# A four-layer fp32 decoder trunk on one core: outputs of a state-space block moved into the gated product, and masked attention products of both halves made ahead

## The chip, the core and the metric

The kernel runs on one core of a Trainium2 chip. The core has five engines with their own instruction queues: TensorE (PE, matrix products; its weight loads are shown as PEld), VectorE (DVE), ScalarE (ACT), GpSimd (POOL) and SyncE (SP, which only issues transfers here). They meet through semaphores; PE writes to PSUM, where this kernel keeps eight tiles of 128 x 512 fp32; all else lies in SBUF or in the chip's memory. The metric is the device time of one execution in microseconds. Before the change the median of three runs is 1496.48 us (1496.17 to 1499.66).

## The reference

256 positions of width 1024 pass four layers. Each layer is `h += mixer(rmsnorm(h))`, then `h += relu(rmsnorm(h) @ w1)**2 @ w2` of width 4096, then `h += (p[i] @ ple_proj) * sigmoid(rmsnorm(h) @ ple_gate)`, the embedding step. The mixers are S5, forgetting attention (FoX), gated linear attention (GLA), and S5 again. All is fp32.

S5, cut to what matters:

```python
u = xn @ w_in                              # 64 groups of 16 channels, 64 complex states each
h[t] = a * h[t-1] + bbar @ u[t]            # diagonal, complex, per group
y[t] = Re(C @ h[t]) + d_skip * u[t]
z1, z2 = split(gelu(y) @ w_glu)            # 1024 -> 2 x 1024
out = (z1 * sigmoid(z2)) @ w_out
```

GLA works in four chunks of 64 positions, four heads:

```python
att = where(causal, q_dec @ k_inv.T, 0)    # in the chunk
o = att @ v + q_dec @ state
state = exp(b_last) * state + k_upd.T @ v
out = (rmsnorm(o) * gn * silu(r)) @ w_out
```

## The kernel before

**Dense products.** An fp32 operand is split into a high and a low part (type fp32r in the trace); a product is three matmuls (hi hi, hi lo, lo hi). Weights come in units of 512 KB: SP loads `raw` (a ring of 3 buffers), ACT rounds it to `whi`, DVE subtracts to `wlo` (rings of 4), and PE makes 24 matmuls of 128x256 of it (lines 172 to 174).

**S5** works on four blocks of 256 channels. For block b the step letters are: `w` the input product, `u` and its rearrangement U by 8 small transfers (`s5_inputs`); `i` the block's tables (rotation `rot`, input weights `win`) and the decay; `o` the way out (`qo`), the lag products `pk` (lines 917 to 922, PSUM tag mk), their copy `kk` by ACT, and four transfers that spread it to the lag matrix `tm` (line 932, queue of ACT in the first S5); `s` the state: products of U (line 967, 64x64 matmuls, in pairs for the two halves of the partitions), then on DVE rotations, two scans and the terms P and W (lines 980 to 989); `y` the outputs (`s5_outputs`): py (tag po) sums U against tm (line 1000), P and W against qo (line 1004), then ACT's gelu G (line 1007), four transposes into pg (line 1010), and the split into the two parts of `gT[b]` (lines 266 and 267). `p` is the layer's embedding product, of nothing but inputs.

The first S5 makes its tables in place and keeps P and W apart; the last one fetches tables that were made ahead in earlier layers (`kept`) and adds W into P on DVE (lines 987 to 989). After the steps comes the gated product of gT with `s_w_glu`: for each half, four units of the right columns (sigmoid by ACT), then four of the left. The first S5 runs from 0 to some 188 us, GLA from some 780 to 885, the last S5 from some 1125 to 1260.

**What sets the order.** The strings FIRST and LATER set the program order of the steps. The framework then reorders the instructions of each engine by its own estimate of when their inputs are ready; within an engine they run in the order so found. `issue_after` holds an instruction behind another: the gated product's `wlo` is held behind `lo_after`, the last state row W of the latest block. PSUM is shared by tags with a ring each: acc 3, wk 3, po 1, mk 1; a tile waits until the one before it in the ring has been read. mk holds both the lag products and the transposes of the outputs.

**GLA.** For each half (two chunks): pa = masked products (line 648, 16 records in the trace), `att` from it (POOL's memset, line 650; DVE's predicated copy, line 651), then for both pairs of heads po = att v (line 661) + q state (line 663), and the state update pu (line 669, DVE 675). The square sums of po go by ACT (681) and POOL (682, 683) to DVE's o (686).

Of the kernel before, what the change touches and what calls it, by code (L numbers as in the profile page):

```python
# [13 lines left out]
ALU = mybir.AluOpType  # L14
# [3 lines left out]
T, D, FF, DEPTH = 256, 1024, 4096, 4  # L18
# [4 lines left out]
        "acc": 3, "wk": 3, "po": 1, "mk": 1}  # L23


FIRST = "f0 w0 o0 w1 i0 w2 w3 f1 s0 i1 o1 s1 f2 i2 y0 o2 s2 y1 f3 i3 o3 s3 y2 p0 y3"
LATER = "w0 i0 o0 w1 i1 o1 w2 s0 i2 w3 s1 y0 o2 s2 i3 y1 o3 s3 y2 p3 y3"

HELD = 2

# [28 lines left out]
class Trunk:  # L59


    def __init__(self, ctx, tc, A):
        self.tc, self.nc, self.A = tc, tc.nc, A
        nc = self.nc
# [4 lines left out]
        self.dram = pool("dram", bufs=1, space=bass.MemoryType.DRAM)  # L69
        self.sm = pool("sm", bufs=4)  # L70
        self.pp = pool("pp", bufs=4, space=PSUM)
        self.kept = self.ahead = self.last_unit = self.lo_after = None
        self.pp_done = {}
        P = 128
        const = lambda name, shape, dt=F32: self.const.tile(shape, dt, name=name)
# [72 lines left out]
    def unit(self, src, nk, nc_, scale=None):  # L148

        nc = self.nc  # L150
        raw = self.wp.tile([128, nk, nc_], F32, name="raw", tag="raw", bufs=BUFS["raw"])
        self.last_unit = nc.sync.dma_start(raw, src.rearrange("(k p) n -> p k n", p=128))
        hi = self.wp.tile([128, nk, nc_], F32R, name="whi", tag="wh", bufs=BUFS["wh"])
        lo = self.wp.tile([128, nk, nc_], F32R, name="wlo", tag="wl", bufs=BUFS["wl"])
        if scale is None:
            nc.scalar.copy(hi, raw)  # L156
            with self.tc.issue_after(self.lo_after.ins) if self.lo_after else nullcontext():
                self.last_lo = nc.vector.tensor_tensor(lo, raw, hi.bitcast(F32), ALU.subtract)  # L158
        else:
            nc.scalar.mul(hi, raw, scale)  # L160
            nc.vector.scalar_tensor_tensor(lo, raw, scale, hi.bitcast(F32), ALU.mult, ALU.subtract)
        return hi, lo
# [412 lines left out]
    def gla(self, l):  # L575
        nc, A = self.nc, self.A
        NH, DK, DV = 4, 128, 256
        x = self.scaled(l)
# [8 lines left out]
        r = self.rstd(rows)  # L587
# [15 lines left out]
        last = chunks(cum)[:, :, :, 63:64]  # L603
# [35 lines left out]
        self.dense(x, A["gla_w_in"], key, (1,), tags=("acc", "wk"))  # L639
        state = [self.a2("state", (128, 2, DV)) for b in range(2)]  # L640
        os = [[None, None], [None, None]]
        for half in range(2):
            pa = self.psum((128, NH, 64))
            for h in range(NH):
# [4 lines left out]
            at = self.t2("att", (128, NH, 64))  # L649
            nc.gpsimd.memset(at, 0.0)  # L650
            nc.vector.copy_predicated(at, self.causal.bitcast(mybir.dt.uint8), pa)
            for b in range(2):
                po = self.psum((128, 2, DV))
                for c in range(2):
                    cs = slice(c * 64, (c + 1) * 64)
                    ts = slice(half * 128 + c * 64, half * 128 + (c + 1) * 64)
                    first = half == 0 and c == 0
# [9 lines left out]
                    for hh in range(2):  # L667
                        h = 2 * b + hh
                        nc.tensor.matmul(pu[:, hh, :], ku[half][cs, h * DK:(h + 1) * DK], v[half][b][cs, hh * DV:(hh + 1) * DV],
                                         start=True, stop=True)  # L670
# [285 lines left out]
    def s5_states(self, b, U, win, rot, d0, split):  # L956

        nc = self.nc
        V = nc.vector
# [21 lines left out]
        if split:  # L981
            V.memset(W[:, :, :, 0:1], 0.0)
            V.tensor_tensor(W[:, 0, :, 1:64], r[:, 1], s, ALU.mult)
            self.lo_after = V.scalar_tensor_tensor(W[:, 1, :, 1:64], r[:, 0], -1.0, s, ALU.mult, ALU.mult)
            return U, [[P[:, i], W[:, i]] for i in range(2)]
        w = W[:, :, :, 1:64]
        V.tensor_tensor(w, r, s.unsqueeze(1).broadcast_to([128, 2, 8, 63]), ALU.mult)
# [4 lines left out]
    def s5_outputs(self, b, U, terms, out, tm, gT):  # L992

        nc = self.nc

        py = self.psum((128, 8, 64), "po")
        gs = [slice(g * 64, (g + 1) * 64) for g in range(2)]
        for p in range(8):
            for g in range(2):
                nc.tensor.matmul(py[gs[g], p, :], U[gs[g], p, :], tm[gs[g], p], start=True, stop=False, skip_group_check=True)  # L1000
            for i in range(2):
                for n, t in enumerate(terms[i]):
                    for g in range(2):
                        nc.tensor.matmul(py[gs[g], p, :], t[gs[g], p, :], out[i][gs[g], :, p], start=False, stop=i == 1 and n == len(terms[i]) - 1,
                                         skip_group_check=True)
        G = self.t2("G", (128, 4, 8, 16))
        nc.scalar.activation(G, py.rearrange("x p (i c) -> x i p c", i=4), AF.Gelu_apprx_tanh)
        pg = self.psum((128, 2, T), "mk")
        for i in range(4):
            nc.tensor.transpose(pg[:, :, i::4], G[:, i].rearrange("x p c -> x (p c)"), self.ident)  # L1010
        self.split(pg, gT[b][:, :, 0], gT[b][:, :, 1])
# [29 lines left out]
    def s5(self, l):  # L1041
# [71 lines left out]

        for t in (FIRST if first else LATER).split():
            step(t[0], int(t[1]))
        if first:
            self.masks()
        m = self.ktiles("glu", tag="m4")
        for b in range(2):
            sg = [None, None]  # L1120

            def right(n, ps):
                sg[n % 2] = self.f2("sg")
                nc.scalar.activation(sg[n % 2], ps, AF.Sigmoid)

            def left(n, ps):
                t = sg[n % 2]
                nc.vector.tensor_tensor(t, ps, t, ALU.mult)
                self.split(t, m[n][:, :, 0], m[n][:, :, 1])

            self.dense(gT, A["s5_w_glu"][j], right, (b + 2,))
            self.dense(gT, A["s5_w_glu"][j], left, (b,))
        self.lo_after = None
        self.out_proj(m, A["s5_w_out"][j])

    def final(self, out):
# [96 lines left out]
```

## Time and profile before

| | |
|---|---|
| median of 3 runs | 1496.48 us (1496.17 to 1499.66) |
| profiled execution | 1498.76 us, of it the span 1497.0 us |
| mean granted TensorE clock | 0.971 of full |
| busy: PE, PEld, DVE, ACT, POOL | 95%, 85%, 70%, 48%, 6% |
| instructions | 26616 |
| memory traffic | 242.68 MB read, 7.86 MB written, 167 GB/s over the span |

The span goes from the first to the last instruction of the profiled execution. In a timeline a row is a run of like instructions: start, busy time, engine, line, operation, tiles written and read, shape, count; in brackets stands how long the engine had idled before and what ended it. An fp32 matmul shows as two records. Waits are put down to the event that came last. An answer by stretches gives, for each, its length, then busy time and instruction count of the engines, the granted clock, the share of the transfer engines and GB/s.

### The profile page before, as it was taken

Reading aid. Unit: us, or ns where it says so; the run is one execution under the profiler, and the core shown is the slowest. Engines: PE = TensorE matmul, PEld = TensorE weight load, DVE = VectorE, ACT = ScalarE, POOL = GpSimd, SP = SyncE. Lnnn points to the kernel's source line nnn. Section 1 sums busy time; section 2 is a strip of 40 time slices with the busy share of each in tenths; the row PEclk is TensorE's granted clock in tenths of the full one; section 3 lists DMA queues with packets and bytes.
Section 4 is the critical chain, followed back from the end, with each engine's and each line's share of the span. In section 5 each row is a group of like instructions: output and inputs, shape, how many; then the busy total and the mean of one; then the engine's idle time right before and its main releaser. Section 6 shows DMA issues by size and latency. Waiting matters only on the chain.

```text
span 1497.0 us, 26616 instructions
## 1 busy us (share of the span) xinstructions
PE 1416.0 (95%) x10734; PEld 1273.0 (85%) x10734; DVE 1055.2 (70%) x1739; ACT 721.3 (48%) x1118; POOL 85.7 (6%) x142
## 2 busy tenths in 40 slices
PE   8767999999999999999999999999999699999998
PEld 7656998888999888887999568888899699888898
DVE  8973477786776678886776528887666956766765
ACT  3212455455565555454567425545554244554444
POOL 3100000000100000010004000000000000000020
PEclk9979999999999999999999969999999899999999
DMA  6503565556645446775564415676576445566562
GB/s 223 167 13 92 185 184 180 180 173 228 186 138 158 141 127 188 247 232 183 182 186 137 154 43 182 220 230 205 170 247 200 123 138 176 169 204 187 169 197 71
DMA packets 146347, 255.06 MB, mean 170 GB/s; under 512 B 24768, under 2 KB 35296, under 8 KB 146224
## 3 DMA queue, kind: packets, MB, share of 16 engines
q1 hardware_dynamic: 132912, 234.35, 50.8%
q0 software_dynamic: 5248, 17.31, 3.5%
q10 hardware_dynamic: 8064, 1.71, 0.6%
q8 instruction: 84, 1.38, 0.4%
q14 instruction: 39, 0.32, 0.1%
HBM read 242.68 MB, written 7.86 MB: 167 GB/s over the span
## 4 chain that ended last, share of the span: by engine, by line
PE 82%; DVE 8%; DMA 4%; ACT 3%; issue 2%; ACTq 0%; POOL 0%; SPq 0%; DVEq 0%; POOLq 0%
PE wk L208 11%; PE acc L208 9%; PE acc L172 6%; PE acc L173 6%; PE acc L174 6%; PE wk L210 5%; PE acc L210 4%; PE wk L172 4%; PE wk L173 4%; PE wk L174 4%; PE mk L208 3%; PE po L208 3%; DVE wlo L158 2%; PE mk L210 2%; PE po L210 1%
## 5 line engine op out<-in xcount | busy, mean ns | idle before, releaser
L158 DVE TENSOR_TENSOR wlo<-raw,whi 128x1024 fp32r<-128x1024 f32 x406 | 494.8, 1228 | 305.3 <-ACT whi L156 298.7
L156 ACT CAST whi<-raw 128x1024 fp32r<-128x1024 f32 x406 | 422.1, 1049 | 464.7 <-PE acc L173 85.0
L208 PE MATMUL wk<-x,whi 128*128 128x512 f32 x576 | 181.2, 399 | 8.3 <-DVE relu L219 8.3
L210 PEld LDWEIGHTS wk<-x,wlo 128*128 128x128 f32 x576 | 106.3, 189 | 23.1 <-issue 0.2
L208 PE MATMUL acc<-s,whi 128*128 128x512 f32 x384 | 118.8, 395 | 0.0
L210 PE MATMUL wk<-x,wlo 128*128 128x256 f32 x576 | 112.9, 280 | 0.0
L172 PE MATMUL acc<-x,whi 128*128 128x256 f32 x352 | 99.6, 288 | 4.6 <-DVE u L1051 2.9
L208 PEld LDWEIGHTS wk<-x,whi 128*128 128x128 f32 x576 | 91.2, 190 | 11.9 <-DVE relu L219 9.2
L173 PE MATMUL acc<-x,whi 128*128 128x256 f32 x352 | 100.4, 288 | 0.0
L174 PE MATMUL acc<-x,wlo 128*128 128x256 f32 x352 | 100.1, 286 | 0.0
L210 PEld LDWEIGHTS acc<-s,wlo 128*128 128x128 f32 x384 | 70.6, 188 | 15.9
L208 PE MATMUL mk<-x,whi 128*128 128x512 f32 x256 | 81.3, 395 | 0.0
L210 PE MATMUL acc<-s,wlo 128*128 128x256 f32 x384 | 74.9, 280 | 0.0
L172 PEld LDWEIGHTS acc<-x,whi 128*128 128x128 f32 x352 | 67.5, 194 | 6.3 <-issue 4.1
L174 PE MATMUL wk<-s,wlo 128*128 128x256 f32 x256 | 72.4, 283 | 0.0
L173 PE MATMUL wk<-s,whi 128*128 128x256 f32 x256 | 72.4, 283 | 0.0
L172 PE MATMUL wk<-s,whi 128*128 128x256 f32 x256 | 72.4, 283 | 0.0
L173 PE MATMUL acc<-g,whi 128*128 128x256 f32 x256 | 72.3, 283 | 0.0
L172 PE MATMUL acc<-g,whi 128*128 128x256 f32 x256 | 72.2, 284 | 0.0
L174 PE MATMUL acc<-g,wlo 128*128 128x256 f32 x256 | 71.7, 283 | 0.0
L174 PEld LDWEIGHTS acc<-x,wlo 128*128 128x128 f32 x352 | 68.2, 194 | 0.1
L173 PEld LDWEIGHTS acc<-x,whi 128*128 128x128 f32 x352 | 68.0, 194 | 0.2
(392 smaller groups left out, 3427.7 us busy)
## 6 DMA issues: line engine op xcount, KB each, us to landing
raw<-mlp_w SPq DMA_DIRECT2D x256, 512.0 KB, 4.1
raw<-s_w_glu SPq DMA_DIRECT2D x32, 512.0 KB, 3.9
raw<-ple_gate SPq DMA_DIRECT2D x32, 512.0 KB, 3.7
raw<-fox_w_in SPq DMA_DIRECT2D x24, 512.0 KB, 3.8
raw<-gla_w_in SPq DMA_DIRECT2D x24, 512.0 KB, 3.7
raw<-s_w_out SPq DMA_DIRECT2D x16, 512.0 KB, 3.9
kept<-kept SPq DMA_DIRECT2D x12, 512.0 KB, 5.3
raw<-s_w_in SPq DMA_DIRECT2D x11, 512.0 KB, 5.0
```

What stands on the lines that cost most here:

```text
L156: nc.scalar.copy(hi, raw)
L158: self.last_lo = nc.vector.tensor_tensor(lo, raw, hi.bitcast(F32), ALU.subtract)
L172: mm(ps, hi, x[:, 0], start=first, stop=False, skip_group_check=True)
L173: mm(ps, hi, x[:, 1], start=False, stop=False, skip_group_check=True)
L174: self.last_mm = mm(ps, lo, x[:, 0], start=False, stop=last, skip_group_check=True)
L208: mm(ps[n], hi[:, i, s], v[i], start=first and i == 0, stop=False, skip_group_check=True)
L210: self.last_mm = mm(ps[n][:, 0], lo[:, i, s], v[i][:, 0], start=False, stop=last and i == UK - 1, skip_group_check=True)
```

## The change

- The embedding product moves up: behind the state of block 1 (`s1`) in both strings.
- The last outputs, `y3`, leave the strings. They are done inside the first product of the gated layer (`mid={2: rest}`: behind its third unit), whose first three units need only gT[0] to gT[2]. The right columns of the first half take PSUM tag wk, those of the second acc.
- `s5_outputs` makes all matmuls of U first, then all of P, then all of W, not block row by block row; only the first matmul starts the bank and only the last stops it.
- The transposes go to tag acc, not mk.
- `lo_after` is a list. The first gated units' `wlo` is held behind block 2's W; from `rest` on behind block 3's.
- `masks()`, two constants on POOL for later layers, is called behind the gated loop.
- GLA makes pa and att of both halves before the first po.

```diff
-FIRST = "f0 w0 o0 w1 i0 w2 w3 f1 s0 i1 o1 s1 f2 i2 y0 o2 s2 y1 f3 i3 o3 s3 y2 p0 y3"
-LATER = "w0 i0 o0 w1 i1 o1 w2 s0 i2 w3 s1 y0 o2 s2 i3 y1 o3 s3 y2 p3 y3"
+FIRST = "f0 w0 o0 w1 i0 w2 w3 f1 s0 i1 o1 s1 p0 f2 i2 y0 o2 s2 y1 f3 i3 o3 s3 y2"
+LATER = "w0 i0 o0 w1 i1 o1 w2 s0 i2 w3 s1 p3 y0 o2 s2 i3 y1 o3 s3 y2"
...
-            with self.tc.issue_after(self.lo_after.ins) if self.lo_after else nullcontext():
+            with self.tc.issue_after(self.lo_after[0].ins) if self.lo_after else nullcontext():
...
+        att = []
         for half in range(2):
             pa = self.psum((128, NH, 64))
...
             nc.vector.copy_predicated(at, self.causal.bitcast(mybir.dt.uint8), pa)
+            att.append(at)
+        for half in range(2):
+            at = att[half]
             for b in range(2):
                 po = self.psum((128, 2, DV))
...
-            self.lo_after = V.scalar_tensor_tensor(W[:, 1, :, 1:64], r[:, 0], -1.0, s, ALU.mult, ALU.mult)
+            last = V.scalar_tensor_tensor(W[:, 1, :, 1:64], r[:, 0], -1.0, s, ALU.mult, ALU.mult)
+            self.lo_after.append(last)
...
-        for p in range(8):
-            for g in range(2):
-                nc.tensor.matmul(py[gs[g], p, :], U[gs[g], p, :], tm[gs[g], p], start=True, stop=False, skip_group_check=True)
-            for i in range(2):
-                for n, t in enumerate(terms[i]):
-                    for g in range(2):
-                        nc.tensor.matmul(py[gs[g], p, :], t[gs[g], p, :], out[i][gs[g], :, p], start=False, stop=i == 1 and n == len(terms[i]) - 1,
-                                         skip_group_check=True)
+        def add(x, w, start=False, stop=False):
+            for p in range(8):
+                for g in range(2):
+                    nc.tensor.matmul(py[gs[g], p, :], x[gs[g], p, :], w[gs[g], :, p] if w is not tm else w[gs[g], p], start=start and p == 0,
+                                     stop=stop and p == 7, skip_group_check=True)
+
+
+        add(U, tm, start=True)
+        parts = [(t[n], out[i]) for n in range(len(terms[0])) for i, t in enumerate(terms)]
+        for n, (t, w) in enumerate(parts):
+            add(t, w, stop=n == len(parts) - 1)
...
-        pg = self.psum((128, 2, T), "mk")
+        pg = self.psum((128, 2, T), "acc")
...
-        if first:
-            self.masks()
...
+            def rest():
+                self.s5_outputs(3, *states[3], *outs[3], gT)
+                self.lo_after = self.lo_after[-1:]
+
+            self.lo_after = self.lo_after[-2:]
+            self.dense(gT, A["s5_w_glu"][j], right, (b + 2,), mid={2: rest} if b == 0 else None, tags=("wk", "wk") if b == 0 else ("acc", "acc"))
             self.dense(gT, A["s5_w_glu"][j], left, (b,))
-        self.lo_after = None
+        self.lo_after = []
+        if first:
+            self.masks()
```

How the engines' orders move is seen at three places. In the rows a name's number tells one buffer from another; lines behind some 640 are a few higher in the changed kernel.

PE in the first S5, at the lag products of block 2 (tag mk). Before, they stand in the middle of block 1's outputs:

```order
L1004 MATMUL po_976<-qo_603,W_717 64x64 x2
L1000 MATMUL po_976<-tm1_107,U_409 64x64 x2
L1004 MATMUL po_976<-qo_603,P_716 64x64
L917 LDWEIGHTS zero_102
L917 MATMUL mk_869<-zero_102 32x512
```

With the change they follow block 0's outputs, which follow the embedding product:

```order
L454 MATMUL acc_751<-praw_731,raw_748 128x256 x4
L454 MATMUL acc_757<-praw_731,raw_748 128x256 x4
L1007 MATMUL po_790<-tm0_106,U_331 64x64 x10
L1007 MATMUL po_790<-qo_340,P_572 64x64 x32
L1007 MATMUL po_790<-qo_340,W_573 64x64 x32
L922 LDWEIGHTS zero_102
L922 MATMUL mk_901<-zero_102 32x512
L925 MATMUL mk_901<-qo_880,bx_896 32x64 x11
L1019 MATMUL acc_873<-ident_84,G_871 128x128 x4
```

The embedding product moved from behind y2 to before y0, the lag products of block 2 from y1 to right behind y0, and y0's transposes (acc_873) into them.

DVE in the first S5, at the end of block 1's state. Before, block 0's state ends here, and the scratch of block 2's tables stands among its rows:

```order
L976 SCALAR_TENSOR_TENSOR R_571<-decay_418,R_571 128x512 x2
L982 MEMSET W_573 128x16
L704 TENSOR_TENSOR scratch_1077<-F1_239,F8_240 128x512 x2
L703 TENSOR_TENSOR bc_1071<-bc_1071,coef_191 128x128
L705 TENSOR_TENSOR bb_1098<-bb_1098 128x128
L704 TENSOR_TENSOR bc_1071<-bc_1071,coef_191 128x128
L705 TENSOR_TENSOR R_715<-R_715,W_717 128x512 x2
L1065 MEMSET decay_587 128x8
L984 SCALAR_TENSOR_TENSOR W_573<-R_571,rot_421 128x8x63
```

With the change, block 1's state runs to its end and the tables `rot` of blocks 2 and 3 follow:

```order
L981 SCALAR_TENSOR_TENSOR R_715<-decay_587,R_715 128x512 x2
L987 MEMSET W_717 128x16
L989 SCALAR_TENSOR_TENSOR W_717<-R_715,rot_590 128x8x63
L985 TENSOR_TENSOR P_716<-R_715,rot_590 128x16x63
L988 TENSOR_TENSOR W_717<-R_715,rot_590 128x8x63
L708 TENSOR_TENSOR rot_773<-F1_239,F8_240 128x512 x2
L708 TENSOR_TENSOR rot_1108<-F1_239,F8_240 128x512 x2
L710 TENSOR_TENSOR rot_773<-rot_773,scratch_774 128x512 x2
```

The tables moved behind the states; the three first `wlo` of the gated product, which stood behind block 3's W row, now stand behind block 2's.

PE in GLA, from the first half to the second (att_8694 and att_8642 are the second half's). Before:

```order
L663 MATMUL wk_8659<-state_8620,e1_8168 64x256
L661 MATMUL wk_8659<-v_8199,att_8630 64x256
L663 MATMUL wk_8659<-state_8620,e1_8168 64x256
L648 MATMUL wk_8685<-e1_8168,e2_8169 64x64 x8
L661 MATMUL wk_8697<-v_8200,att_8694 64x256
L663 MATMUL wk_8697<-state_8619,e1_8168 64x256
```

With the change:

```order
L668 MATMUL wk_8671<-state_8620,e1_8168 64x256
L666 MATMUL wk_8671<-v_8199,att_8630 64x256
L668 MATMUL wk_8671<-state_8620,e1_8168 64x256
L666 MATMUL wk_8697<-v_8200,att_8642 64x256
L668 MATMUL wk_8697<-state_8619,e1_8168 64x256
```

The second half's masked products (L648, L650 in the changed kernel) left this place and stand with the first half's, among dense products.

More of the change, by code (lines that the diff above doesn't have):

```diff
@@ L71, in __init__ @@
         self.pp = pool("pp", bufs=4, space=PSUM)
-        self.kept = self.ahead = self.last_unit = self.lo_after = None
+        self.kept = self.ahead = self.last_unit = None
+        self.lo_after = []
         self.pp_done = {}
@@ L1129, in left @@
                 self.split(t, m[n][:, :, 0], m[n][:, :, 1])
-            self.dense(gT, A["s5_w_glu"][j], right, (b + 2,))
+            def rest():
[3 more added lines that the diff above has]
+            self.dense(gT, A["s5_w_glu"][j], right, (b + 2,), mid={2: rest} if b == 0 else None, tags=("wk", "wk") if b == 0 else ("acc", "acc"))
             self.dense(gT, A["s5_w_glu"][j], left, (b,))
-        self.lo_after = None
+        self.lo_after = []
+        if first:
+            self.masks()
         self.out_proj(m, A["s5_w_out"][j])
```

## The prediction

> **What bounds the kernel now.** I read the page first, then the waits of TensorE (PE) by stage, then the timeline of the places where they are long.
>
> ```profile
> PE 1416.0 (95%) x10734; PEld 1273.0 (85%) x10734; DVE 1055.2 (70%) x1739; ACT 721.3 (48%) x1118; POOL 85.7 (6%) x142
> ```
>
> PE is the bound: 81 us of the 1497.0 us span are all that it idles. A change that only moves work, as this one does, can win those and the time in which PE runs on a low clock, nothing else. The waits up to 145 us, with engine, tile and line, what ended them, sum, times and longest:
>
> ```profile
> PE mk L917 <- DVE g L267: 11.1, 2, 10.0
> PE po L1004 <- DVE P L980: 7.4, 1, 7.4
> PE mk L1010 <- ACT G L1007: 5.8, 1, 5.8
> ```
>
> These three, 24.3 us, are all in the first S5. PE's timeline there (start, duration, what ended the idle time in brackets), and VectorE's (DVE):
>
> ```profile
> 78.21 0.48 PE L1004 MATMUL po<-qo,P 64*64 64x64 f32 x4 [7.41 <-DVE P L980]
> ...
> 98.53 0.58 PE L917 MATMUL mk<-zero 1*32 1x512 bf16 x1 [10.00 <-DVE g L267]
> 99.05 3.62 PE L920 MATMUL mk<-qo,bx 128*32 128x64 f32 x32
> ...
> 141.94 0.39 PE L172 MATMUL acc<-g,whi 128*128 128x256 f32 x1
> ```
>
> ```profile
> 78.06 0.69 DVE L983 TENSOR_TENSOR W<-R,rot 128x504 f32<-128x504 f32 x1
> ...
> 97.79 0.69 DVE L267 TENSOR_TENSOR g<-mk,g 128x512 fp32r<-128x512 f32 x1
> 108.31 0.68 DVE L704 TENSOR_TENSOR W<-acc,rot 128x512 f32<-128x512 f32 x1 [9.83 <-PE acc L967]
> ...
> 116.43 0.68 DVE L983 TENSOR_TENSOR W<-R,rot 128x504 f32<-128x504 f32 x1
> ```
>
> It is a ring. The lag products of block 2 need bank mk, which the transposes of block 0 hold until DVE has split them (97.79); DVE is busy with three blocks' states until then; then DVE starves for 9.83 us, since block 3's products stand behind on PE. The first gated matmul starts at 141.94, 25 us after the last state row (116.43).
>
> **The change part by part.** The prices of the pieces come from one answer by stretches (length, then busy time of PE, PEld, DVE, ACT and POOL, granted clock): products of a block, lag products, transposes, outputs of a block, gated product:
>
> ```profile
> 47.58:51.45 3.87, 3.87 (x129) 3.80 (x128) 3.87 (x7) 0.00 (x0) 1.55 (x3) 1.00 0.47 143
> 51.45:54.44 2.99, 2.74 (x39) 2.06 (x35) 2.99 (x10) 0.00 (x0) 0.00 (x0) 1.00 0.90 269
> 86.21:86.80 0.59, 0.59 (x7) 0.42 (x5) 0.59 (x2) 0.00 (x0) 0.00 (x0) 1.00 0.00 0
> 136.96:141.94 4.98, 4.98 (x159) 4.91 (x158) 0.00 (x0) 0.58 (x1) 0.00 (x0) 0.96 0.71 253
> 145.00:180.00 35.00, 35.00 (x294) 35.00 (x293) 17.89 (x17) 17.50 (x20) 0.00 (x0) 1.00 0.54 165
> ```
>
> 35.0 us / 294 is 0.119 us a matmul, so a gated unit of 24 takes 2.87 us and three 8.6.
>
> *First S5.* With the transposes in an acc bank, the lag products of block 2 wait for DVE's qo alone. The order of DVE has changed with it: the state of block 1 now stands ahead of the rotation tables and qo of block 2. Up to block 0's last W (78.75) DVE sheds twelve 128x512 operations of 0.60 us and five small ones of 0.2, 8.2 us, and takes up block 1's two scans, P and two W halves, 4.6 us: block 1 ends at 75.1 where DVE never waits. Ten more 128x512 operations (tables, scratch, qo) make 6.0: PE can start the lag products at 81. Against that, PE now has 21 of block 0's products before the last two input blocks and waits there for wl; following the rows by hand this costs DVE 5 us. I take the late end, 86. From there PE has, up to the point where three gated units, y3 and its transposes are done, 2 lag products, 2 blocks of products, 3 outputs, 4 sets of transposes, 3 units: 5.5 + 7.7 + 14.9 + 2.4 + 8.6 = 39.1 us. PE will have idled some 8 us before, so the lag products run at half rate, as from 98.53 on (to the end of the matmuls of 99.05 and the short one behind them 4.6 us, against 2.74): +1.9. The end is 127.0. Before, the same point is 141.94 + 8.6 + 0.6 = 151.1. Gain 24.1; start at 81 makes it 29. For semaphores that a hand count misses I take 2 off: **22**. Splitting y into all U, all P and all W matmuls changes their order, not their number.
>
> What hides the rest: y3 needs block 3's last W. DVE has no row more up to there than before but three wlo (1.2 us each), and the 9.83 us starve falls away, so W is ready by about 117 at worst, 4 us before PE comes to y3 (127.0 - 0.6 - 4.98). If that cover is gone, each us late is a us of PE. The three wlo ahead of P delay y2 by 3.5 us, under block 3's products. The embedding product (16 matmuls, in the wait before y0) also frees its two raw buffers 60 us earlier, so the three first gated weights are there.
>
> *Gated linear attention.* PE's timeline, before the wait and behind it:
>
> ```profile
> 853.22 0.65 PE L663 MATMUL wk<-state,e 128*64 128x256 f32 x2
> 853.80 0.64 PE L661 MATMUL wk<-v,att 64*64 64x256 f32 x2
> ...
> 858.81 1.11 PE L661 MATMUL wk<-v,att 64*64 64x256 f32 x2 [3.33 <-DVE att L651]
> 859.85 1.11 PE L663 MATMUL wk<-state,e 128*64 128x256 f32 x2
> ...
> 876.62 1.09 PE L273 MATMUL wk<-ident,silu 128*128 128x128 f32 x4 [1.21 <-DVE o L686]
> ...
> 882.53 0.79 PE L172 MATMUL acc<-o,whi 128*128 128x256 f32 x2 [0.64 <-ACT o L266]
> ```
>
> ```profile
> 854.20:857.60 3.40, 1.28 (x20) 0.89 (x18) 1.87 (x4) 1.70 (x5) 1.34 (x3) 1.00 0.01 2
> 861.00:864.40 3.40, 3.40 (x7) 1.63 (x8) 0.00 (x0) 0.00 (x0) 0.00 (x0) 0.50 0.02 5
> 884.70:888.10 3.40, 3.40 (x18) 3.40 (x18) 0.89 (x3) 0.37 (x1) 0.11 (x1) 0.50 0.50 154
> 1164.97:1168.38 3.41, 2.01 (x64) 1.88 (x64) 3.41 (x5) 0.00 (x0) 0.00 (x0) 1.00 0.46 141
> ```
>
> The wait is 3.33 us, but it costs more: behind it a pair starts every 1.04 us where it took 0.58, with the granted clock at 0.50 for 30 us though PE is busy all the time. Small matmuls of 64 rows or columns do not bring the clock back; the dense ones of the output projection do (888). With both halves' att made ahead, no att is waited for there. At full rate the stretch 858.81 to 882.53, 21.9 us without the waits of 1.21 and 0.64, takes 0.56 of it: -9.6. The dense start, about 5 us at half rate, wins 2. The wait wins 3.3; the state updates that it hid come out, and I put them at 1.5, a little under those two other waits: **13.5** in all, if the clock holds. The last row shows a stretch of 64x64 matmuls, busy 59%, that kept it. If it falls all the same at 857 to 861, the wait and 2 to 5.5 us at full rate are left: 3.3 - 1.5 + 1.6 to 4.3, so 3 to 6.
>
> [...]
>
> *Last S5.* Its waits are shorter:
>
> ```profile
> PE po L1004 <- DVE P L988: 6.4, 2, 6.0
> PE acc L967 <- DMA kept<-kept: 4.3, 2, 2.9
> ```
>
> ```profile
> 1202.95 0.68 DVE L989 TENSOR_TENSOR P<-P,W 128x504 f32<-128x504 f32 x1
> 1203.54 0.69 DVE L267 TENSOR_TENSOR g<-mk,g 128x512 fp32r<-128x512 f32 x1
> 1204.14 2.35 DVE L158 TENSOR_TENSOR wlo<-raw,whi 128x1024 fp32r<-128x1024 f32 x2
> ```
>
> DVE sets the end here, and the change puts two wlo (2.35) ahead of its last blocks: last P at about 1206, the split of block 2's transposes, which the third unit needs, one wlo and one split later, 1207.8. Then 22 matmuls (2.6), 26 of y3 (1.5), G and transposes (1.3): 1213.2. Before: the gated product starts at 1206.4, so 1206.4 + 8.6 + 0.6 = 1215.6. Gain **2**. On SyncE's queue two raw loads, which wait for wlo, now stand ahead of block 3's kept tables: up to 3 lost. If the whole wait for P went, it would be 6.4 won.
>
> Sum: 22 + 13.5 + 2 = 37.5 off the profiled 1498.76 us, 1461.3; the median of the runs is 2.3 lower: **1459 us**.
>
> **The rivals.** *The clock falls in the attention all the same*: its small matmuls fill the array too little. For it speaks 861.00 to 864.40, busy and not restored; against it that falling and returning may need different amounts of work (the row at 59%). Gain 5 there: 1467.5.
>
> *The first S5 gives half*: DVE rows or a U or tm transfer, not bank mk, hold PE, and the wait comes back at qo of block 2. For it: DVE is without a pause from 56 to 98 us. Gain 11 there: 1470, or 1478 with the low clock.
>
> *No net change*: the wait for mk becomes a wait of the gated product for y3, and the attention's for state: 1492 to 1501.
>
> *Slower*: y3 now stands in PE's queue in the middle of the gated product, and needs tm of block 3, whose copy stands on ACT behind a weight cast that waits for a load. Before, this row held it:
>
> ```profile
> 119.66 1.04 ACT L156 CAST whi<-raw 128x1024 fp32r<-128x1024 f32 x1 [10.56 <-DMA raw<-s_w_glu]
> ```
>
> The new order ends y3 about 5.6 us after its inputs (4.98 + 0.6), so first S5 is no shorter once tm comes later than 145.5, and the whole is slower by more than 4.5 us, with nothing won elsewhere, from 150. I expect tm at about 109; 40 us more are four such waits in a row.
>
> **How the numbers follow.** Chances: forecast 0.45 (1452 to 1466 by itself), low clock 0.25, half 0.20, no change 0.05, slower 0.05. 1448 to 1480 takes in the first two, the high end of the first S5's gain (29 instead of 22, 1452, with 4 more from the last S5) and most of the third. A measurement of this kernel tells 0.3%, 4.5 us, from no change: faster 0.90, within 0.05, slower 0.05.
>
> **What would show it.** First S5: no wait for a split g ahead of the lag products; one wait for qo of block 2 ending between 81 and 86; the first gated matmul ahead of y3, at about 112; y3 without a wait. If P or W is waited for at y3, DVE's order was too slow. Attention: no wait for att; clock 1.00 until the output projection, which starts 12 us or more nearer to the input products. A clock of 0.50 there means the first rival. Last S5: two gated units on PE ahead of block 3's last P, and no wait for kept over 6 us. The forecast is wrong if a first-S5 wait of over 10 us on DMA or ACT appears.

## The result, and the profile after

The median falls from 1496.33 (with a fourth run of the kernel before; the first three gave 1496.48) to 1457.97 us (1456.13 to 1461.99): a ratio of 0.9742, 95% interval 0.9715 to 0.9769, 38 us. The forecast was 1459 us. The profiled execution took 1461.99 us, of it 1460.2 us the span, 36.8 us less than the one before; the sum of the prediction had put it at 1461.3 us.

The page of the changed kernel has the same work on every engine, so what was won is idle time of PE, 81 to 56 us, and time in which it ran at a low clock, 12 us less busy for the same matmuls (mean granted clock 0.984 instead of 0.971):

```profile
PE 1403.9 (96%) x10734; PEld 1266.9 (87%) x10734; DVE 1054.3 (72%) x1739; ACT 723.2 (50%) x1118; POOL 86.8 (6%) x142
```

Where the time went is read from SyncE's queue. The loads of the weights run ahead by a fixed ring, so the start of the first load of a weight marks a stage. Before (start, length, queue, line, transfer):

```profile
173.72 6.08 SPq L152 DMA_DIRECT2D raw<-s_w_out  x3
...
752.04 76.73 SPq L152 DMA_DIRECT2D raw<-gla_w_in  x24
894.24 4.93 SPq L152 DMA_DIRECT2D raw<-mlp_w  x2
...
1116.93 7.19 SPq L152 DMA_DIRECT2D raw<-s_w_in  x3
...
1238.18 11.84 SPq L152 DMA_DIRECT2D raw<-s_w_out  x5
```

After:

```profile
150.28 21.73 SPq L153 DMA_DIRECT2D raw<-s_w_out  x8
...
728.15 76.67 SPq L153 DMA_DIRECT2D raw<-gla_w_in  x24
855.30 42.89 SPq L153 DMA_DIRECT2D raw<-mlp_w  x15
1077.60 7.19 SPq L153 DMA_DIRECT2D raw<-s_w_in  x3
...
1201.31 21.73 SPq L153 DMA_DIRECT2D raw<-s_w_out  x8
```

The first S5 (from 0 to the first `s_w_out`) lost 23.4 us, the GLA stage (`gla_w_in` to `mlp_w`) went from 142.20 to 127.15, so 15.05 less, and the last S5 (`s_w_in` to `s_w_out`) from 121.25 to 123.71, so 2.5 **more**. The rest changed by 0.8 us in sum. Two of the three parts did what was forecast; the third went the other way. These are single profiles, and both S5 stages vary from one to the next, as the table of the experiments shows.

**First S5.** PE's waits up to 145 us, those that belong to the change:

```profile
PE acc L454 <- DVE R L708: 3.9, 1, 3.9
PE mk L925 <- DVE qo L710: 3.7, 3, 2.8
...
PE po L1007 <- issue: 2.0, 1, 2.0
```

Of the three waits of 24.3 us in all, 0.7 us for G is left; in their place stand 3.7 us for `qo`, 3.9 us of the embedding product, whose bank (tag acc) DVE had not yet read out for block 1's state, and 2.0 us in block 2's outputs that end with nothing the profile shows ("issue"). PE's timeline has the lag products of block 2, the first gated matmul, and the transposes of block 3:

```profile
82.82 0.30 PE L925 MATMUL mk<-qo,bx 128*32 128x64 f32 x2 [2.77 <-DVE qo L710]
...
111.91 0.39 PE L173 MATMUL wk<-g,whi 128*128 128x256 f32 x1
...
127.17 0.66 PE L1019 MATMUL acc<-ident,G 128*128 128x128 f32 x4 [0.69 <-ACT G L1016]
```

**GLA.** All of PE's waits between 760 and 880 us, and a stretch behind the place of the old wait (length, busy times of PE, PEld, DVE, ACT, POOL, granted clock, transfers):

```profile
PE acc L173 <- ACT o L267: 1.1, 1, 1.1
PE wk L668 <- DVE state L680: 0.6, 1, 0.6
```

```profile
834.00:840.00 6.00, 5.43 (x20) 2.17 (x20) 2.35 (x5) 0.95 (x4) 0.92 (x3) 1.00 0.28 90
```

No `att` is waited for, and the same small matmuls that ran at 0.50 before now run at 1.00.

**Last S5.** The two stretches that the low clock spoils, the embedding product and the third gated unit:

```profile
1133.40:1145.70 12.30, 12.28 (x104) 11.01 (x104) 11.54 (x16) 2.61 (x4) 0.00 (x0) 0.66 0.45 148
```

```profile
1170.00:1176.00 6.00, 5.37 (x29) 5.15 (x30) 1.71 (x2) 0.49 (x1) 0.00 (x0) 0.50 0.53 175
```

The transposes of block 3, at which the prediction had measured this stage, on PE's timeline:

```profile
1178.21 0.66 PE L1019 MATMUL acc<-ident,G 128*128 128x128 f32 x4 [0.70 <-ACT G L1016]
```

DVE from block 1's last state row (the second of its two subtractions of W, `P<-P,W`) to block 2's, before and after:

```profile
1182.08 0.68 DVE L989 TENSOR_TENSOR P<-P,W 128x504 f32<-128x504 f32 x1
...
1192.22 0.68 DVE L989 TENSOR_TENSOR P<-P,W 128x504 f32<-128x504 f32 x1
```

```profile
1143.11 0.68 DVE L995 TENSOR_TENSOR P<-P,W 128x504 f32<-128x504 f32 x1
1144.04 1.22 DVE L159 TENSOR_TENSOR wlo<-raw,whi 128x1024 fp32r<-128x1024 f32 x1 [0.25 <-ACT whi L157]
1146.79 1.22 DVE L159 TENSOR_TENSOR wlo<-raw,whi 128x1024 fp32r<-128x1024 f32 x1 [1.52 <-ACT whi L157]
...
1158.04 0.68 DVE L995 TENSOR_TENSOR P<-P,W 128x504 f32<-128x504 f32 x1
```

It took 10.1 us and takes 14.9. The two `wlo` are about 2.4 us of the difference, as forecast; the other half is time in which DVE stands still. The rows put 1.77 us of that to ACT's `whi`; what would have held DVE even without that wait, the experiments show.

### The profile page after: what moved, and what is told of

Its sections match the earlier page's. It is cut to its first block, busy times and chain, and to the rows that moved or that the text cites. A ratio compares the mean times of both kernels' runs of the same rounds, so it can differ in the third digit from the quotient of the medians.

```text
span 1460.2 us, 26622 instructions
## 1 busy us (share of the span) xinstructions
PE 1403.9 (96%) x10734; PEld 1266.9 (87%) x10734; DVE 1054.3 (72%) x1739; ACT 723.2 (50%) x1118; POOL 86.8 (6%) x142
## 5 line engine op out<-in xcount | busy, mean ns | idle before, releaser
L209 PEld LDWEIGHTS wk<-x,whi 128*128 128x128 f32 x576 | 92.2, 192 | 11.5 <-DVE relu L220 8.6
L209 PEld LDWEIGHTS acc<-s,whi 128*128 128x128 f32 x384 | 59.6, 189 | 1.4
L209 PE MATMUL po<-s,whi 128*128 128x512 f32 x192 | 60.7, 396 | 0.0
L209 PE MATMUL wk<-s,whi 128*128 128x512 f32 x192 | 60.1, 395 | 0.0
```

Source lines behind the costliest of these rows:

```text
L209: mm(ps[n], hi[:, i, s], v[i], start=first and i == 0, stop=False, skip_group_check=True)
```

## The experiments

For each kernel the table gives the median, its ratio to the kernel before with the 95% interval, and from its profiled execution the three stages as read above. The kernel before, run again beside each group of them, has medians of 1495.1 to 1496.3 us.

| kernel | median us | ratio | first S5 | GLA | last S5 |
|---|---|---|---|---|---|
| before | 1496.33 | 1 | 173.72 | 142.20 | 121.25 |
| changed | 1457.97 | 0.9742 (0.9715 to 0.9769) | 150.28 | 127.15 | 123.71 |
| GLA loop undone | 1472.97 | 0.9848 (0.9816 to 0.9879) | 153.08 | 142.70 | 124.13 |
| GLA loop alone | 1483.59 | 0.9918 (0.9903 to 0.9933) | 171.08 | 127.26 | 120.88 |
| old GLA loop, wait filled | 1463.40 | 0.9780 (0.9760 to 0.9800) | 146.35 | 131.93 | 124.67 |
| GLA, short wait left | 1474.80 | 0.9864 (0.9848 to 0.9881) | 147.01 | 142.74 | 122.07 |
| transposes back in mk | 1465.06 | 0.9791 (0.9775 to 0.9807) | 154.78 | 126.60 | 118.83 |
| transposes in acc alone | 1492.51 | 0.9971 (0.9954 to 0.9988) | 163.01 | 141.28 | 125.84 |
| embedding product back | 1466.02 | 0.9805 (0.9789 to 0.9821) | 158.15 | 128.00 | 119.82 |
| y3 back ahead (first S5) | 1457.61 | 0.9750 (0.9735 to 0.9766) | 146.46 | 127.09 | 125.55 |
| matmuls by block row | 1460.34 | 0.9763 (0.9748 to 0.9777) | 146.25 | 126.73 | 127.70 |
| last S5 undone | 1458.13 | 0.9751 (0.9731 to 0.9772) | 146.14 | 126.56 | 127.28 |
| last S5, wlo late | 1457.63 | 0.9752 (0.9729 to 0.9776) | 144.12 | 126.59 | 124.85 |
| last S5, waits filled | 1457.86 | 0.9744 (0.9729 to 0.9760) | 147.11 | 127.03 | 124.78 |

The columns repeat well where the code of a stage is the same: GLA is 126.6 to 128.0 with the new loop and 141.3 to 142.7 with the old one. The two S5 stages do not: the first gave 144.1 to 153.1 in the seven kernels that have it as changed, the last 119.8 to 125.6 in six. A single profile therefore says nothing about 5 us in these stages, and what follows on them goes by the medians, or by waits that come and go. Two parts of the change were never taken back by themselves: the new place of `masks()`, and the earlier `wlo` of the first S5.

### GLA: what the wait cost, and why

The loop undone in the changed kernel, and put alone into the kernel before:

```diff
-        att = []
         for half in range(2):
             pa = self.psum((128, NH, 64))
...
             nc.vector.copy_predicated(at, self.causal.bitcast(mybir.dt.uint8), pa)
-            att.append(at)
-        for half in range(2):
-            at = att[half]
             for b in range(2):
```

> The changed kernel with the linear attention as before: each half's masked products and att made just ahead of its own use. Theory (the 3.3 us wait for att lets PE's clock fall, and the small matmuls behind it do not bring it back): a wait of about 3.3 us for att returns, the granted clock is 0.50 for some 30 us behind it, and the time goes up by about 15 us, to 1473. Rival (only the wait itself counts, the clock loss would come anyway or is made good later): 3 to 5 us more, 1461 to 1463.

> The kernel before with only the linear attention changed (att of both halves ahead). Theory: the parts add up, so about 15 us less than before, 1481, with the clock at 1.00 through the attention. [...]

Undone, 15.0 us come back; alone, the loop wins 11.5 us in the median and 14.9 in the profile's stage. The wait and the low clock return together. The undone kernel's wait, and a stretch behind it:

```profile
PE wk L662 <- DVE att L652: 3.3, 1, 3.3
```

```profile
840.00:846.00 6.00, 6.00 (x15) 2.08 (x14) 0.87 (x2) 0.00 (x0) 0.00 (x0) 0.50 0.00 0
```

The next kernel keeps the old loop and its late `att`, and gives PE something to do: 14 dense matmuls whose sums nobody reads.

```diff
+            if half:
+                fill = self.psum((128, 2, T), "mk")
+                with self.tc.issue_after(tail.ins):
+                    for n in range(14):
+                        nc.tensor.matmul(fill, x[0][:, 0, 0, 0:128], x[0][:, 0], start=True, stop=True)
             for b in range(2):
...
-                            nc.tensor.matmul(po[cs, hh, :], e1[:, h, ts], state[b][:, hh, :], start=False, stop=True)
+                            tail = nc.tensor.matmul(po[cs, hh, :], e1[:, h, ts], state[b][:, hh, :], start=False, stop=True)
```

> As the run with the attention undone, but PE makes 14 dense matmuls of 128x512, whose sums nobody reads, in the place of the wait for att (extra work). Theory (idleness is what costs the clock): the wait shrinks to under 1 us, the clock stays at 1.00, and the time is that of the changed kernel and the 3.3 us of filler, 1461 to 1463, though it does more work than the run without filler. Rival (the small matmuls themselves lower the clock once they run alone for a few us): the clock falls all the same and the time is 1470 or more.

Its timeline row of the added work, and the stretch behind it:

```profile
827.25 3.47 PE L657 MATMUL mk<-x 128*128 128x512 f32 x14
```

```profile
830.70:836.00 5.30, 5.30 (x22) 2.15 (x22) 1.35 (x3) 0.00 (x0) 0.00 (x0) 1.00 0.15 54
```

So `att` is as late as before, PE does 3.5 us more work, and the stage still falls from 142.7 to 131.9 us. Some 11 of the 15 us were the clock, and the wait itself only the rest. The small matmuls of this stage kept a clock of 1.00 once they had it (830.70 to 836.00 here); they only failed to bring it back (0.50 all through 840 to 846 us with the loop undone).

How short must a wait be? In the changed kernel the second half's `att` was held behind the first half's last state update:

```diff
-            nc.vector.copy_predicated(at, self.causal.bitcast(mybir.dt.uint8), pa)
+            if half == 0:
+                nc.vector.copy_predicated(at, self.causal.bitcast(mybir.dt.uint8), pa)
...
         for half in range(2):
             at = att[half]
+            if half:
+                with self.tc.issue_after(late.ins):
+                    nc.vector.copy_predicated(at, self.causal.bitcast(mybir.dt.uint8), last_pa)
...
-                            nc.vector.scalar_tensor_tensor(state[b][:, hh, :], ...)
+                            late = nc.vector.scalar_tensor_tensor(state[b][:, hh, :], ...)
```

> The changed kernel, but att of the second half is copied only after the last state update of the first half, so that PE waits some 1 to 2 us for it instead of not at all (3.3 before). [...] Rival (in this stretch of small matmuls any wait is enough): clock 0.50 behind it and 1468 or more.

The rival's number came: the median is 1474.80, 16.8 us above the changed kernel, as if nothing had been won. PE's timeline has a wait of 1.51 us for `state` and then one of 1.31 for `att`; the stretch around the first one is given below it:

```profile
827.55 0.77 PE L673 MATMUL wk<-state,e 128*64 128x256 f32 x2 [1.51 <-DVE state L682]
828.25 1.11 PE L671 MATMUL wk<-v,att 64*64 64x256 f32 x2
...
833.72 1.11 PE L671 MATMUL wk<-v,att 64*64 64x256 f32 x2 [1.31 <-DVE att L661]
```

```profile
824.40:827.80 3.40, 1.89 (x9) 0.98 (x7) 1.82 (x2) 1.23 (x2) 0.00 (x0) 1.00 0.46 157
```

The pair of 828.25 is already at half rate, so the wait of 1.51 us was enough here; the `att` wait came when the clock had fallen. In the 3.40 us ahead of the fall PE was busy for 1.89 us, 56%; in the row that the prediction quoted as kept it was 2.01 us of 3.41, 59%. In the kernel before, the stretch ahead of the fall had 1.28 us of work by the prediction's row (854.20 to 857.60). In the traces of the kernel before and of the changed one, the end of an execution aside, the granted clock is 1.00 or 0.50 for a whole multiple of 3.41 us (0.50 for 30.72 us, nine times that, in this stage of the kernel before).

The busy share alone does not settle it. Taken in the trace's own stretches of 3.41 us, two of the first S5 in the kernel before kept the clock with less than those 56%, 1.56 us of work (46%, 120.31 to 123.72) and 1.69 us (50%), and one of the last S5 with its waits filled lost it with 2.17 us (64%, 1130.25 to 1133.66). The row of the 50%:

```profile
69.11:72.52 3.41, 1.69 (x58) 1.56 (x52) 3.41 (x8) 1.53 (x2) 0.00 (x0) 1.00 0.25 48
```

Nor is it the count of 64 rows or columns that kept the clock from coming back, as the prediction had it. The outputs of S5 in the kernel before are 64x64 matmuls with 64 columns moving, issued in pairs for the two halves of the partitions; one full stretch of them brought it back:

```profile
79.35:82.76 3.41, 3.41 (x70) 3.41 (x68) 3.41 (x7) 0.00 (x0) 0.00 (x0) 0.50 0.02 5
82.76:86.17 3.41, 3.41 (x118) 3.38 (x114) 3.41 (x6) 0.89 (x2) 0.00 (x0) 1.00 0.02 5
```

What sets the matmuls of GLA apart from these is not shown.

### First S5: which part of the change wins

Five kernels take back one part each, or do one alone. The transposes' tag, in the changed kernel and (reversed) in the kernel before:

```diff
-        pg = self.psum((128, 2, T), "acc")
+        pg = self.psum((128, 2, T), "mk")
```

> The changed kernel with the transposes of the outputs back in bank mk. Theory (one bank for lag products and transposes is what made the ring of waits): PE must bring block 0's transposes, their copy and split to an end before block 2's lag products, so a wait of some us for G or the split g comes back in the first S5: 1461 to 1468. Rival (the gain of the first S5 comes from the early embedding product and the later y3, not from the bank): 1457 to 1459.

> The kernel before with one edit: the transposes go to the acc ring. Theory (the 10 us wait at the lag products and DVE's starving go, but y3 and the embedding product still stand ahead of the gated product, and raw buffers are held): 5 to 12 us less than before, 1484 to 1491. Rival (the bank is all of the first stage's gain): 1473. Other rival (the wait only moves to the next thing that DVE owes): 1494 to 1497.

With mk the old wait is back on PE, though shorter, and the kernel is 7 us slower in the median (the edit sets the tag in both S5 stages):

```profile
PE mk L922 <- DVE g L268: 10.1, 2, 6.5
```

Alone, acc wins 3.4 us of the median (1495.95 for the kernel before beside it), between the two expectations. The first S5 of its profile is 8 to 11 us shorter than the old one, and in it the wait has partly moved: the transposes now wait for G on ACT, and the lag products for `qo`.

```profile
PE acc L1010 <- ACT G L1007: 8.5, 3, 7.1
...
PE mk L920 <- DVE qo L705: 4.1, 1, 4.1
```

The last S5 of the same profile is 4.6 us longer than before. The new tag seems to have a price there; the kernel with the last S5 undone shows a wait of this kind below.

The embedding product put back behind y2, in FIRST only:

```diff
-FIRST = "f0 w0 o0 w1 i0 w2 w3 f1 s0 i1 o1 s1 p0 f2 i2 y0 o2 s2 y1 f3 i3 o3 s3 y2"
+FIRST = "f0 w0 o0 w1 i0 w2 w3 f1 s0 i1 o1 s1 f2 i2 y0 o2 s2 y1 f3 i3 o3 s3 y2 p0"
```

> The changed kernel with the first embedding product behind y2 again. Theory (its place sets the order of the input products and frees two of three weight buffers, so the gated weights would come late and y0 with it): the first gated weights are waited for or ACT's queue stands on one, 4 to 15 us more, 1462 to 1473. Rival (it only fills a wait on PE and any place does): 1457 to 1460.

It costs 8 us of the median, and its trace says how. The transposes of block 1 wait for G, and on ACT the row of G stands behind a weight cast, which waits for a load that has no free raw buffer: SyncE's loads of the gated weights go on at 95.65, where the changed kernel has 70.47. PE's longest wait, and ACT's timeline:

```profile
PE acc L1019 <- ACT G L1016: 10.5, 2, 9.8
```

```profile
99.48 1.04 ACT L157 CAST whi<-raw 128x1024 fp32r<-128x1024 f32 x1 [12.53 <-DMA raw<-s_w_glu]
100.43 0.59 ACT L1016 ACTIVATE G<-po 128x512 f32<-128x512 f32 x1
```

The raw buffers are what the early embedding product gives back. The 8 us are put down to that here; what its 16 matmuls win by filling a wait was not tried by itself.

The part that gives the change its name, y3 inside the gated product, undone in the first S5, and the new order of the output matmuls undone in both:

```diff
-FIRST = "... y1 f3 i3 o3 s3 y2"
+FIRST = "... y1 f3 i3 o3 s3 y2 y3"
...
-            self.dense(..., mid={2: rest} if b == 0 else None, ...)
+            self.dense(..., mid={2: rest} if b == 0 and not first else None, ...)
```

> The changed kernel, but in the first S5 y3 stands ahead of the gated product again. Theory (block 3's last W comes at 112.7 us, soon after y2's end at 111.9, and 21 gated matmuls fill the gap, so little is left to hide): 0 to 3 us more, 1458 to 1461. Rival (putting y3 inside the gated product carries a good part of the first stage's gain): 5 us more or beyond, 1463 and up.

> The changed kernel with the output matmuls in their old order: for each of eight block rows U, then P and W by turns. Theory (order without number, and P and W are both there when PE comes to them): within 1.5 us of the changed kernel, 1456.5 to 1459.5. Rival (taking U and P first lets y start before W is there): 3 us more or beyond.

Neither shows in the median: 1457.61 and 1460.34 us against 1457.97, with intervals that overlap; 1460.34 lies between its two expectations. Without the ring of waits block 3's W is ready when y3 comes, with y3 in either place: PE does not wait ahead of it in either trace.

### Last S5: why nothing was won

The last S5 put back into its old order (strings, y3 ahead of the gated product), with the tag acc and the new matmul order kept:

```diff
-LATER = "w0 i0 o0 w1 i1 o1 w2 s0 i2 w3 s1 p3 y0 o2 s2 i3 y1 o3 s3 y2"
+LATER = "w0 i0 o0 w1 i1 o1 w2 s0 i2 w3 s1 y0 o2 s2 i3 y1 o3 s3 y2 p3 y3"
...
+            self.lo_after = self.lo_after[-2:] if first else self.lo_after[-1:]
+            self.dense(..., mid={2: rest} if first and b == 0 else None, ...)
```

> The changed kernel with the last S5 in its old order: embedding product behind y2, y3 ahead of the gated product, its right columns in acc; only the transposes' bank and the order of the output matmuls stay changed there. Theory (the change loses about 2.5 us in the last S5, because two low parts of gated weights, and the waits for their high parts, stand on DVE ahead of the last blocks' states): 1455 to 1456. Rival (the 2.5 us are made elsewhere, by the way the stretch before it ends): 1458.

The median is the same, at the rival's number, and the theory's 1455 to 1456 was missed; the stage is no shorter. DVE's states are back where they were, though: block 2's takes 10.2 us again, so it is the new order that delays them. But the kernel is no clean return. In the old order the embedding product stands between the transposes, and now both use acc: its third bank waits until DVE has split block 2's transposes. PE's timeline:

```profile
1159.77 0.39 PE L173 MATMUL acc<-p,whi 128*128 128x256 f32 x1 [3.86 <-DVE g L268]
```

So the tag acc does not go with the old place of that product. With the new place, two suspects are left, `wlo` on DVE and the clock. `wlo` first: in both kernels `lo_after` is empty in the last S5, so nothing holds them there. Here, from the third gated unit on, the low parts of the weights are held behind block 3's last P.

```diff
-            with self.tc.issue_after(self.lo_after[0].ins) if self.lo_after else nullcontext():
+            self.seen += 1
+            with self.tc.issue_after(self.lo_after[0].ins) if self.lo_after and self.seen > self.free else nullcontext():
...
-        V.tensor_tensor(P[:, 1, :, 1:64], P[:, 1, :, 1:64], w[:, 0], ALU.subtract)
+        self.lo_after.append(V.tensor_tensor(P[:, 1, :, 1:64], P[:, 1, :, 1:64], w[:, 0], ALU.subtract))
...
-            self.lo_after = self.lo_after[-2:]
+            self.lo_after = self.lo_after[-2:] if first else self.lo_after[-1:]
+            if b == 0:
+                self.seen, self.free = 0, 0 if first else 2
```

> The changed kernel with one edit in the last S5: from the third gated unit on, the low part of the weights is held on DVE behind block 3's last P. Theory (the two low parts ahead of block 2's and 3's states cost DVE 4.5 us there, and the idle time that follows on PE lowers its clock): block 3's last P comes 3 to 4.5 us earlier, the fall of the clock behind it goes or shrinks, 1453 to 1456. Rival (the split of block 2's transposes or the weights' transfer sets the end): 1457 to 1459.

No difference in the median, and block 2's state takes 14.9 us as in the changed kernel. DVE's timeline shows why: in the place of the two `wlo` it now idles, for block 2's state products on PE.

```profile
1136.74 0.68 DVE L997 TENSOR_TENSOR P<-P,W 128x504 f32<-128x504 f32 x1
1140.71 1.29 DVE L710 TENSOR_TENSOR R<-wk,kept 128x512 f32<-128x512 f32 x2 [3.30 <-PE wk L974]
```

PE was busy with the embedding product, which the change put ahead of them, among block 0's outputs; in the changed kernel that stretch ran at 0.66 of the clock behind the wait for P. The kernel with the embedding product put back in the first S5 has the same source for the last one, but there the clock over that product was 0.79, and DVE hardly stands still:

```profile
1139.10:1149.70 10.60, 10.53 (x105) 9.53 (x105) 10.53 (x16) 2.62 (x4) 0.00 (x0) 0.79 0.40 120
```

```profile
1149.36 0.68 DVE L995 TENSOR_TENSOR P<-P,W 128x504 f32<-128x504 f32 x1
1149.95 2.35 DVE L159 TENSOR_TENSOR wlo<-raw,whi 128x1024 fp32r<-128x1024 f32 x2
1152.22 1.28 DVE L708 TENSOR_TENSOR R<-wk,kept 128x512 f32<-128x512 f32 x2
...
1162.06 0.68 DVE L995 TENSOR_TENSOR P<-P,W 128x504 f32<-128x504 f32 x1
```

12.7 us between the first and the last of these rows are about the old 10.1 and the two `wlo`, and the stage is 119.82, 1.4 less than before: there the forecast gain of 2 nearly came. The kernel with the transposes in mk is the other one of this kind (12.7 and 118.83). In both the clock was back at 1.00 59.1 us into the stage, in the middle of the embedding product. The changed kernel and four more with the same source for this stage (three with an edit to GLA, one with y3 put back in the first S5) had it back only after 64 to 67 us; block 2's state took 14.6 to 15.5 us in them, and the stage 122.1 to 125.6.

The clock last: 32 more dense matmuls whose sums nobody reads, in the two waits.

```diff
+    def fill(self, x, n, after):
+        ps = self.psum((128, 2, T), "mk")
+        with self.tc.issue_after(after.ins):
+            for _ in range(n):
+                self.nc.tensor.matmul(ps, x[:, 0, 0, 0:128], x[:, 0], start=True, stop=True)
...
+                if b == 1 and not first:
+                    self.fill(x[0], 18, self.s_mm)
...
+        if fill:
+            self.fill(gT[0], fill, self.y_mm)
...
-                self.s5_outputs(3, *states[3], *outs[3], gT)
+                self.s5_outputs(3, *states[3], *outs[3], gT, fill=0 if first else 14)
```

> The changed kernel with 32 more dense 128x512 matmuls in the last S5, whose sums nobody reads: 18 in the wait of block 0's outputs for P (5.1 us), 14 in the waits of block 3's outputs (2.0 and 1.8 us). By the 14 that took 3.47 us in the attention they take 4.5 and 3.5 us. Theory (the last S5 loses its gain to the clock, which falls in these waits and leaves the embedding product and the third gated unit at 0.50): the clock stays at 1.00 there, the time from the first load of s_w_in to the first of s_w_out falls from 122 to 125.5 us (as the kernels with this last S5 have it) to 118 to 121, the median from 1458 to 1453 to 1456 us. Rival (DVE's rows alone set the end): clock 1.00, but the stretch stays at 122 to 125.5 and the median at 1457 to 1460. If the added matmuls hold PE up: 1460 to 1464.

The clock held through the first wait, by the stretch that holds the fill:

```profile
1123.90:1129.90 6.00, 5.09 (x45) 3.92 (x40) 6.00 (x8) 1.24 (x2) 0.00 (x0) 1.00 0.52 125
```

Nothing else came as the theory had it: the stage (124.78) and the median (1457.86) stay, and DVE's two rows are 14.8 us apart, where the changed kernel has 14.9.

```profile
1139.61 0.68 DVE L995 TENSOR_TENSOR P<-P,W 128x504 f32<-128x504 f32 x1
...
1154.42 0.68 DVE L995 TENSOR_TENSOR P<-P,W 128x504 f32<-128x504 f32 x1
```

The test did not hold the clock where it was meant to. Small waits came back among block 0's outputs, the clock fell at 1133.66, behind a stretch in which PE was busy for 2.17 us of 3.41, and the embedding product ran into it:

```profile
1130.25:1133.66 3.41, 2.17 (x14) 1.48 (x15) 3.41 (x8) 0.00 (x0) 0.00 (x0) 1.00 0.59 190
```

From the first of block 0's outputs to block 2's state products PE took 12.4 us, and 12.5 in the changed kernel (1133.42 to 1145.96):

```profile
1129.92 0.33 PE L1013 MATMUL po<-kept,P 64*64 64x64 f32 x2 [0.93 <-DVE P L994]
...
1142.31 1.45 PE L972 MATMUL wk<-U,kept 64*64 64x64 f32 x44
```

The rival's numbers came out, then, but the test does not decide for it. Shown, by the return to the old order and by the kernel with `wlo` late, is that the second half of DVE's delay comes with the new order: block 2's products stand behind the embedding product, and DVE would wait for them with or without the two `wlo`. That the low clock makes the difference between 12.7 and some 15 us rests on the seven profiles above, not on an edit, and how much of it the place alone costs stays open. The next thing to try would be mk for the transposes of the last S5 and acc for the first; it was not tried. No kernel tried beats the changed one by more than its interval.

## Why the prediction was right, and where not

**First S5, 22 us forecast, 23.4 in the profile.** The mechanism held: `qo` of block 2 released the lag products at 82.8 (81 to 86), the first gated matmul came at 111.9 (about 112), y3's transposes ended at 127.8 (127.0), and no wait for block 3's W or its `tm` stands ahead of y3. That the last two times fit so well is luck: the lag products started 3.2 us ahead of the 86 that the sum took, and the way from there took 45.0 us instead of 41.0, with the 2.0 us in block 2's outputs and 3.41 us of half clock behind them (107.6 to 111.0) that the sum did not have. It did not see the 3.9 us that the embedding product waits for its bank either; they set nothing, since PE waits for `qo` behind them all the same. And 23.4 is one profile: over the seven with this first S5, and the two with the old one (171.1 and 173.7), the gain is 18 to 30 us.

But the weights given to the parts were off. The forecast made bank mk the centre and treated the embedding product as a filler that also frees two buffers. Taken back one at a time, the tag costs 7 us and the embedding product 8, each with the rest in place; the tag alone wins 3.4. The mechanism named as the slower rival, a cast on ACT that waits for a load and holds what stands behind it, is real: the prediction's own row of the kernel before has it (10.56 us in front of block 3's copy), and the early embedding product, which frees the buffers, is what removes it (with that product put back there are 12.53 us in front of G). And y3's place in the first S5, whose cover the forecast worked out with care, is worth nothing that the medians can tell.

**GLA, 13.5 us forecast, 15.05 in the profile.** The clock held (1.00 from 834.00 to 840.00), so the rival with 5 us falls; that the small matmuls fill the array too little was its conjecture, which no run shows. The kernel with the wait filled shows that the clock was most of the gain, some 11 us. The term that was mis-sized is the waits, entered as 3.3 won and 1.5 lost, 1.8 in all. Before, PE waited 3.33 + 1.21 + 0.64 = 5.2 us there; now it waits 1.7: 1.1 for ACT's `o`, which is the old 0.64 grown, and 0.6 for `state`, which is new. That is 3.5 won, and 13.5 + 1.7 = 15.2. The reading that small matmuls as such do not bring the clock back was too wide: those of GLA did not (861.00 to 864.40, all busy at 0.50), those of S5 did (79.35 to 82.76 all busy at 0.50, then 1.00).

**Last S5, a gain of 2 forecast, 2.5 lost.** The step that failed is "DVE sets the end here, and the change puts two `wlo` (2.35) ahead of its last blocks": only `wlo` and the kept tables were priced, and the embedding product, which LATER moves as FIRST does, was not. It stood behind block 2's outputs; it stands ahead of block 2's state products now, behind a wait with a low clock after it (0.66 from 1133.40 to 1145.70). Block 2's state takes 4.8 us longer where 2.35 was allowed. y3's transposes end at 1178.87, which on the scale of before (the stage starts 39.33 later there, 1116.93 against 1077.60) is 1218.2, where 1213.2 was forecast and 1215.6 had been; the third unit at 0.50, which took 5.1 us where 2.6 was allowed, adds to it. Two gated units did run ahead of block 3's last P, and the feared wait for kept tables did not come. The loss of 2.5 is one profile too: of the six with this code five are longer than before and one is 1.4 shorter; none has the gain of 2.

The sum was 1461.3 for the profiled execution, against 1461.99: the miss of 4.5 in the last S5 was made up by 1.4, 1.5 and 0.8 us elsewhere, which is luck. The median lies lower than the profile by 4.0 where 2.3 was taken. Of the other rivals, half in the first S5 had its wait for `qo`, but of 2.8 us only; no change and slower have nothing for them in the rows of the changed kernel.

## What to carry to other kernels

Price every instruction that a reordering moves, in every layer that shares the order: work that was cheap in one place is paid in full when it stands ahead of something that another engine waits for. Count for a wait on PE its length and what the clock loses behind it: in GLA 3.3 us, and some 11 more with small matmuls behind it. Making the inputs early removed both; filling the wait with dense work saved the clock in GLA, and did not help in the last S5. Where PE waits for an activation, look at what stands ahead of it on ACT: here a weight cast that waited 12.53 us for a load held the row of G behind it, and an early reader of the raw buffers removed that.

## What the runs showed of the hardware

- In the traces of the kernel before and of the changed one the granted clock is 1.00 or 0.50, each for whole multiples of 3.41 us, the end of an execution aside: 0.50 for 3.41 to 30.72 us at a time before, 3.41 to 10.24 after.
- With a wait of 1.51 us in a stretch of 3.40 us with 1.89 us of work (56%) it fell to 0.50 (GLA, short wait left). The busy share did not decide alone: 1.56 and 1.69 us of work in 3.41 (46 and 50%) kept the clock in the first S5 of the kernel before, 2.17 in 3.41 (64%) lost it in the last S5 with its waits filled.
- The matmuls of GLA kept a clock of 1.00 but did not restore it from 0.50: with PE busy in all of 840 to 846 us it stayed at 0.50 in the kernel with the old loop, and at 1.00 in the same matmuls behind the 14 dense ones (830.70 to 836.00). The 64x64 matmuls of S5, issued in pairs, had it restored: PE busy in all of 79.35 to 82.76 us at 0.50, 1.00 from there, in the kernel before.
- Unchanged code in the first S5 took 144.1 to 153.1 us from one profiled execution to the next, and 119.8 to 125.6 in the last, while the GLA stage kept within 1.4 us.
